# A down projection whose five weight pairs move on one at a time, with loads and epilogues placed by side

## The chip, the cores and the metric

The kernel runs on one core of one Trainium2 chip. The metric is device time in microseconds (us); lower is better. The engines are called PE (matrix multiply), DVE, ACT and POOL, and SP is the engine whose queue issues the transfers. Each engine has a queue of its own and works through it in order; engines wait for each other through semaphores.

## The reference

The program is one layer of a hybrid encoder in float32: a combined input projection, three mixers, an output projection with a norm, and a feed-forward. Only the feed-forward matters here:

```python
D_MODEL, SEQ, D_FF, N_META = 1024, 2048, 2816, 16
f = causal_dwconv(rms_norm(h, norm_ffn_pre[l]) @ ffn_up[l], ffn_conv[l])   # 3 taps
gate, val = jnp.split(f, 2, axis=-1)
f = (jax.nn.gelu(gate, approximate=True) * val) @ ffn_down[l]              # 2816 x 1024
h = h + rms_norm(f, norm_ffn_post[l])
return h[:, N_META:]
```

## The kernel before, in words

Float32 products are made of split operands. An operand is split into a rounded part and the remainder (`split`, L1593 to L1595: a copy on ACT, then a subtraction on DVE or, for some, on POOL), and a product is three matmuls of parts (`mm3`, L172 to L174).

**ffn_up** is the stage ahead. It works in three sweeps ("supers") over the tokens, each with 22 column blocks j. At the end of a block the convolution and the gelu (`conv`, L1723 to L1727, and `ending`, whose multiply is L1731) read the PSUM sums psu, and the result goes to the scratch tensor scr_ff (L1732). Between blocks the function `between` runs work for later; with j = `DOWN_FROM` in the last sweep it loads and splits the first operands of the next stage.

**The down projection** (class `Down` and the block `p4`) multiplies scr_ff by ffn_down. The tokens are cut into 8 pairs of 256. The 2816 rows of the weight are cut into 10 weight pairs of 256 rows (k = 0 to 9) and a rest of 256 rows. Each weight pair is multiplied in a scheme with 7 products in place of 8 (`DOWN_PRODUCTS`), for which both sides are summed in advance. So a weight pair has 7 operands of 128 x 512, each loaded (`down_operands`, L1814, tiles raw; four of the seven are sums that an earlier stage has written to scr_ds), split (on DVE, two of seven on POOL) and kept as a tile of two parts (dw, or qd for nine operands that lie in the memory of the norm's output).

The data side of one weight pair and one token pair is a *side* (`Down.side`): a load u (L1831), four POOL additions (L1838 to L1841), and a split into fo. Then come 21 matmuls, 7 products of 3. One token pair with five weight pairs is a *visit* (`Down.pair`). All 8 PSUM banks belong to this stage.

- First half: 8 visits with k = 0 to 4. All 35 operands stay resident. A visit ends with copies out of PSUM (L1870 to L1872), sums on DVE (L1873 to L1877, L1886) and the stores of the partial result to scr_part (L1894).
- Second half: 8 visits with k = 5 to 9, then the rest (tiles dwn, 24 matmuls). The 35 operands are replaced when the second half begins. The epilogue loads the partial sums (pt, L1881), adds them on POOL (L1883), adds the last PSUM banks (L1886), loads the residual (hx, L1902), applies the norm (`add_normed`, L1507 to L1523) and stores the result (L1904).

The order of instructions on each queue is set by a scheduler, which places each instruction as soon as its estimated inputs are ready; `issue_after` pins an instruction behind another. Pools of tiles are carved from one memory, and a new tile waits for the last readers of the memory that it takes. Raw operands have 8 buffers, u and fo two each, pt and hx together two.

Of the kernel before, what the change touches and what calls it, by code (L numbers as in the profile page):

```python
# [1526 lines left out]

HALO = 2
# [172 lines left out]
DOWN_SLOTS = 5, 13, 8  # L1701
DOWN_TURNS = (2, 3), (0, 5), (1, 13), (2, 5)
DOWN_FROM = 14
# [4 lines left out]
def ffn_up(core, raws, ring, pool, banks, w_up, cw, scr, between, tokens):  # L1708
# [11 lines left out]
    def conv(src, u, j, n):  # L1720
        y = pool.tile([P, FBLK], F32, tag="uy", name=core.n("uy"), bufs=UY)
        cc = u * NFF + j
        nc.scalar.activation(y[:, :n], src[:, 2 : n + 2], AF.Copy, scale=cw[:, 88 + cc : 89 + cc])  # L1723
        for i in (1, 0):
            stt(y[:, :n], src[:, i : n + i], cw[:, 44 * i + cc : 44 * i + cc + 1], y[:, :n], op0=ALU.mult, op1=ALU.add)  # L1725
        if u == 0:
            nc.scalar.activation(y[:, :n], y[:, :n], AF.Gelu_apprx_tanh)  # L1727
        return y
# [5 lines left out]
    for at, (sup, j) in enumerate(units):  # L1734
# [9 lines left out]
        for i, (name, (_, _, at_)) in enumerate(PRODUCTS.items()):  # L1744
# [20 lines left out]
            elif name == "p3":  # L1765
                tt(ps, ps, u2, op=ALU.add)
                gb = conv(ps, 0, j, n[1])
# [3 lines left out]
            elif name == "p2":  # L1771
                tt(ps, ps, ga, op=ALU.add)
                ga = conv(ps, 0, j, n[0])
                ending(gb, vb, j, b0[1], n[1])
            else:
                va = conv(ps, 1, j, n[0])
# [18 lines left out]


# [5 lines left out]
def down_operands(core, raw, slot, w_down, scr, k):  # L1802


    out = []
    for i, (_, s) in enumerate(DOWN_PRODUCTS.values()):
        t = raw()
# [13 lines left out]
class Down:  # L1821
    def __init__(self, core, spool, fpool, epool, psum, scr, gain, out):
        self.core, self.spool, self.fpool, self.epool, self.psum = core, spool, fpool, epool, psum
        self.scr, self.gain, self.out = scr, gain, out

    def side(self, k, pair):
# [4 lines left out]
        nc.sync.dma_start(u[:, 0:4].rearrange("p (j i) t -> p j (i t)", j=2), src.rearrange("(j p) t -> p j t", p=P))  # L1831
        if k == DOWN_PAIRS:
            fo = self.fpool.tile([P, 2, 4, P], F32R, tag="fo", name=core.n("fo"))
            split(core, fo[:, 0], fo[:, 1], u[:, 0:4])
            return {s: (fo[:, 0, i], fo[:, 1, i]) for i, s in enumerate(("b0", "a0", "b1", "a1"))}
        tt = nc.gpsimd.tensor_tensor
        b0, a0, b1, a1, s1, s2, s3, s4 = (u[:, i] for i in range(8))
        tt(s1, b0, b1, op=ALU.add)  # L1838
        tt(s2, s1, a0, op=ALU.subtract)
        tt(s3, a0, b0, op=ALU.subtract)  # L1840
        tt(s4, a1, s2, op=ALU.subtract)  # L1841
        fo = self.fpool.tile([P, 2, 7, P], F32R, tag="fo", name=core.n("fo"))
        split(core, fo[:, 0], fo[:, 1], u[:, 1:8])
        return {s: (fo[:, 0, i], fo[:, 1, i]) for i, s in enumerate(DOWN_SIDE)}
# [4 lines left out]
    def pair(self, pair, ks, weights, rest=None):  # L1849
# [3 lines left out]
        for k in ks:  # L1853
            side, w = self.side(k, pair), weights(k)
# [15 lines left out]
        nc.scalar.activation(la, ps["p1"][:], AF.Copy)  # L1870
# [7 lines left out]
        for i, row in enumerate(((lb, rb), (la, ra)) if rest else ()):  # L1878
            t0 = P * (2 * pair + i)
            pt = self.spool.tile([P, D], F32, tag="hx", name=core.n("pt"))  # L1880
            nc.sync.dma_start(pt[:], self.scr["part"][t0 : t0 + P, :])  # L1881
            for c, y in enumerate(row):
                nc.gpsimd.tensor_tensor(y, y, pt[:, 512 * c : 512 * c + 512], op=ALU.add)  # L1883
# [5 lines left out]
    def first(self, pair, ks, weights):  # L1889
        nc = self.core.nc  # L1890
        for i, halves in zip((1, 0), self.pair(pair, ks, weights)):
            t0 = P * (2 * pair + i)
            for c, y in enumerate(halves):
                nc.sync.dma_start(self.scr["part"][t0 : t0 + P, 512 * c : 512 * c + 512], y)  # L1894

    def second(self, pair, ks, weights, rest):
        core, nc = self.core, self.core.nc
        a, b, junk = self.pair(pair, ks, weights, rest)
        for i, halves in ((1, a), (0, b)):
            t0 = P * (2 * pair + i)  # L1900
            hx = self.spool.tile([P, D], F32, tag="hx", name=core.n("hx"))
# [312 lines left out]
```

## Time and profile before

| | |
|---|---|
| median of 3 runs | 3066.63 us |
| the runs | 3066.63, 3073.84, 3063.35 us |
| profiled execution: span | 3071.8 us (no separate time of it is given; the span is taken as its time) |
| mean granted clock of PE | 0.969 |
| PE busy | 95% of the span |
| matmuls of the down projection | 1872, from 2597.3 to 3060.6 us |

The profile is of one execution. Times within it are counted from the start of the span. The rows of the views follow where the prediction uses them. A row of a table by stretches has the length of the stretch, the busy time of each engine with the number of its instructions, the granted clock of PE (1.00 is full), the mean busy share of the DMA engines, and GB/s. A row of a table of waits has the engine and operation that waited, what it waited for, the total in us, how often, and the longest.

### The profile page before, as it was taken

To read this page: it belongs to the slowest core of one execution; us is meant where nothing else is said; L and a number is where in the kernel's file an instruction comes from. 1 tells how busy PE (TensorE), PEld (TensorE's weight loads), DVE (VectorE), ACT (ScalarE), POOL (GpSimd) and SP (SyncE) were. 2 spreads that over 40 slices of the span, in tenths; PEclk is the share of its full clock that TensorE was granted. 3 is DMA by queue.
4 is the path that set the end of the run, shared out by engine and by line. 5 is a ranking of instruction groups with operands and counts; after the bars stand their busy time and mean duration, and the time that the engine had idled before them with its cause. 6 is when DMAs were issued, how large, how long until landed. Compare 5 with 4: busy or idle time off the path is not lost. (4 is left out here: it accounts for less than half of the span.)

```text
span 3071.8 us, 52793 instructions
## 1 busy us (share of the span) xinstructions
PE 2921.6 (95%) x18694; PEld 2495.2 (81%) x18694; DVE 2054.8 (67%) x3934; ACT 1482.3 (48%) x2853; POOL 1358.8 (44%) x1589
## 2 busy tenths in 40 slices
PE   6999999999989999999989899999999999999998
PEld 6998898888876654665558899999999998787876
DVE  5268645656667785556635788888778786547766
ACT  4245332443336553555534656666566665324333
POOL 1001121122114555667842457445655444547765
PEclk9998999999988898999999999999999999999999
DMA  6776578466654346535245555566777765435444
GB/s 211 244 237 207 161 244 287 156 211 204 196 153 94 88 104 199 133 99 122 62 129 173 168 182 180 169 201 208 214 215 216 219 189 171 161 104 171 149 160 144
DMA packets 467818, 532.58 MB, mean 173 GB/s; under 512 B 85488, under 2 KB 355514, under 8 KB 466000
## 3 DMA queue, kind: packets, MB, share of 16 engines
q1 hardware_dynamic: 467168, 528.81, 56.5%
q8 instruction: 147, 2.41, 0.3%
q14 instruction: 119, 0.97, 0.1%
q0 software_dynamic: 384, 0.39, 0.0%
HBM read 369.11 MB, written 159.95 MB: 172 GB/s over the span
## 5 line engine op out<-in xcount | busy, mean ns | idle before, releaser
L172 PE MATMUL psu<-xo,uw 128*128 128x344 f32 x1848 | 589.9, 323 | 16.7 <-ACT xo L1594 6.9
L173 PE MATMUL psu<-xo,uw 128*128 128x344 f32 x1848 | 592.6, 321 | 0.0
L174 PE MATMUL psu<-xo,uw 128*128 128x344 f32 x1848 | 582.9, 320 | 0.0
L172 PE MATMUL psp<-xh,wh 128*128 128x384 f32 (+2 forms) x1152 | 383.6, 333 | 4.1 <-ACT wh L166 2.4
L174 PE MATMUL psp<-xh,wl 128*128 128x384 f32 (+2 forms) x1152 | 380.7, 331 | 3.5 <-DMA wl<-scr_wk 3.5
L173 PE MATMUL psp<-xl,wh 128*128 128x384 f32 (+2 forms) x1152 | 380.5, 330 | 0.0
L172 PEld LDWEIGHTS psu<-xo,uw 128*128 128x128 f32 x1848 | 346.9, 188 | 20.3 <-ACT xo L1594 7.1
L1595 DVE TENSOR_TENSOR uw<-uq,uw 128x512 fp32r<-128x512 f32 x341 | 316.2, 933 | 70.3 <-ACT uw L1594 63.7
L173 PEld LDWEIGHTS psu<-xo,uw 128*128 128x128 f32 x1848 | 347.9, 188 | 0.3 <-DVE xo L1595 0.3
L174 PEld LDWEIGHTS psu<-xo,uw 128*128 128x128 f32 x1848 | 346.5, 188 | 0.0
L1594 ACT ACTIVATE uw<-uq 128x512 fp32r<-128x512 f32 x462 | 287.9, 627 | 110.1 <-PE psu L174 48.7
L686 ACT ACTIVATE p<-sc,bias 128x512 f32<-128x512 f32 (+4 forms) x352 | 195.8, 590 | 178.5 <-PE sc L682 146.3
L1725 DVE SCALAR_TENSOR_TENSOR uy<-psu,ffn_cols,uy 128x342 f32<-128x342 f32 (+1 forms) x396 | 223.9, 567 | 60.7 <-ACT uy L1723 59.1
L559 DVE TENSOR_REDUCE mc<-mx 128x1 f32<-128x512 f32 (+6 forms) x352 | 190.3, 565 | 100.9 <-PE mx L554 75.8
L1731 POOL TENSOR_TENSOR uy<-uy,uy 128x342 f32<-128x342 f32 (+1 forms) x132 | 140.6, 1065 | 253.2 <-DVE uy L1725 77.4
L725 POOL TENSOR_TENSOR acc<-acc,p 128x512 f32<-128x512 f32 (+3 forms) x208 | 221.8, 1068 | 60.3 <-ACT p L686 23.9
L1595 POOL TENSOR_TENSOR uw<-uq,uw 128x512 fp32r<-128x512 f32 x121 | 177.9, 1470 | 125.0 <-ACT uw L1594 92.7
L174 PEld LDWEIGHTS psp<-xh,wl 128*128 128x128 f32 x1152 | 222.1, 193 | 13.0 <-issue 6.1
L172 PEld LDWEIGHTS psp<-xh,wh 128*128 128x128 f32 x1152 | 222.1, 193 | 10.7 <-issue 4.0
L173 PEld LDWEIGHTS psp<-xl,wh 128*128 128x128 f32 x1152 | 222.1, 193 | 7.6 <-issue 5.5
L1595 DVE TENSOR_TENSOR fo<-u,fo 128x896 fp32r<-128x896 f32 x88 | 112.6, 1279 | 121.3 <-ACT fo L1594 121.3
L1594 ACT ACTIVATE fo<-u 128x896 fp32r<-128x896 f32 x88 | 81.1, 922 | 206.3 <-POOL u L1841 106.8
(465 smaller groups left out, 6470.4 us busy)
## 6 DMA issues: line engine op xcount, KB each, us to landing
uq<-scr_us SPq DMA_DIRECT2D x220, 256.0 KB
uq<-in_ffn_up_dram SPq DMA_DIRECT2D x209, 256.0 KB
wl<-scr_wk SPq DMA_DIRECT2D x48, 512.0 KB
wh<-scr_wk SPq DMA_DIRECT2D x48, 512.0 KB
u<-scr_ff SPq DMA_DIRECT2D x88, 256.0 KB
scr_ff<-uy SPq DMA_DIRECT2D x110, 171.0 KB
raw<-in_w_in_dram SPq DMA_DIRECT2D x24, 512.0 KB
scr_wk<-wh SPq DMA_DIRECT2D x24, 512.0 KB
```

Source lines behind the costliest of these rows:

```text
L172: nc.tensor.matmul(out, ah, bh, start=first, stop=False, skip_group_check=more)
L173: nc.tensor.matmul(out, ah, bl, start=False, stop=False, skip_group_check=more)
L174: nc.tensor.matmul(out, al, bh, start=False, stop=last, skip_group_check=more)
L559: self.reduced = nc.vector.tensor_reduce(mc[:rows, i, ci : ci + 1], ps[:rows, : e - a], axis=AX.X, op=ALU.max)
L686: last = nc.scalar.activation(p[:rows, :w], ps[:rows, :w], AF.Exp, bias=bias[:rows, j : j + 1])
L725: eng.tensor_tensor(a, ps_[0][0][:rows, c0:n] if start and i == 1 else a, p[:rows, : n - c0], op=ALU.add)
L1594: core.nc.scalar.activation(hi, src, AF.Copy)
L1595: (eng or core.nc.vector).tensor_tensor(lo, src, hi, op=ALU.subtract)
L1725: stt(y[:, :n], src[:, i : n + i], cw[:, 44 * i + cc : 44 * i + cc + 1], y[:, :n], op0=ALU.mult, op1=ALU.add)
L1731: core.pooled = nc.gpsimd.tensor_tensor(v[:, :n], g[:, :n], v[:, :n], op=ALU.mult)
```

## The change

The five resident weight pairs become a window that slides. In the first half the windows of the eight visits begin at k = 0, 0, 1, 1, 2, 3, 3, 4, in the second at 5, 5, 6, 6, 7, 8, 8, 9, counted modulo 10; so a token pair p has the same window in both halves, shifted by five, and all ten pairs are used once. One weight pair is replaced at a time: 14 sets of seven operands are loaded and split, where it was 10. A set that the next visit needs is prepared from the third side of the visit before it (`ahead`, `DOWN_AHEAD`), in visits 1, 3, 4, 6, 7, 9, 11, 12 and 14 (of 0 to 15), and its loads are pinned behind the load u of that side.

Further parts:

- Ten operands (all of k = 0, three of k = 1) are prepared in ffn_up, at j = 13 and j = 17 of the last sweep, where it was seven; the tenth lies in the memory of ffn_up's norm gain. The loads of k = 2 and 3 are pinned behind the last convolution (`DOWN_HELD`).
- The convolutions of ffn_up's last block read copies in SBUF, not PSUM; this adds one copy on ACT.
- The weights of the rest are loaded in visit 6.
- Work behind a visit is put off, counted in sides, each piece pinned behind a side's u load: the stores of partial sums by 5, pt's loads and POOL's additions by 2, hx and the norm by 5, the store of the result by 7.
- In the second half the last PSUM banks are added before the stored partial sums instead of after them.
- The norm multiplies by the gain before the root is known, and adds the scaled row into hx in one operation (`add_scaled`).
- The pools of the stage are in another order, and their sizes are 5, 7, 1, 2 and 10 operands beside the nine and the tenth.

```diff
+def add_scaled(core, pool, halves, gain, x, junk):
+
+    nc = core.nc
+    v = pool.tile([P, 8], F32, tag="rs2", name=core.n("rs2"))
+    sums = v[:, 4:5], v[:, 5:6]
+    for y, acc in zip(halves, sums):
+        nc.scalar.activation(junk, y, AF.Square, accum_out=acc)
+    for c, y in enumerate(halves):
+        nc.vector.tensor_tensor(y, y, gain[:, 512 * c : 512 * c + 512], op=ALU.mult)
+    r1 = rstd_root(core, v, sums, D)
+    for c, y in enumerate(halves):
+        xc = x[:, 512 * c : 512 * c + 512]
+        nc.vector.scalar_tensor_tensor(xc, y, r1, xc, op0=ALU.mult, op1=ALU.add)
...
-DOWN_SLOTS = 5, 13, 8
-DOWN_TURNS = (2, 3), (0, 5), (1, 13), (2, 5)
-DOWN_FROM = 14
+DOWN_SLOTS = 5, 7, 1, 2, 10
+DOWN_TURNS = (3, 2), (4, 5), (0, 5), (4, 5), (1, 7), (2, 1)
+DOWN_FROM = 13, 17
+DOWN_HELD = 2, 4
+DOWN_REST = 6
+DOWN_AHEAD = 2
+DOWN_STORED = 5
+DOWN_PARTS, DOWN_NORMS, DOWN_OUT = 2, 5, 7
...
+                sum_ = ps if more else u2
+                tt(sum_, ps, u2, op=ALU.add)
+                gb = conv(sum_, 0, j, n[1])
             elif name == "p7":
                 tt(vb, ps, vb, op=ALU.add)
                 vb = conv(vb, 1, j, n[1])
             elif name == "p2":
-                tt(ps, ps, ga, op=ALU.add)
-                ga = conv(ps, 0, j, n[0])
+                sum_ = ps if more else ga
+                tt(sum_, ps, ga, op=ALU.add)
+                ga = conv(sum_, 0, j, n[0])
                 ending(gb, vb, j, b0[1], n[1])
             else:
-                va = conv(ps, 1, j, n[0])
+                src = ps
+                if not more:
+                    src = s("ga")
+                    nc.scalar.activation(src, ps, AF.Copy)
+                va = conv(src, 1, j, n[0])
...
+def down_visits(pairs):
+
+    for half in range(2):
+        for pair in range(pairs):
+            first = DOWN_CUT * pair // pairs + DOWN_CUT * half
+            yield half, pair, range(first, first + DOWN_CUT)
...
+    def after(self, sides, fn):
+        self.due.append((self.sides + sides, fn))
...
+        self.sides += 1
+        while self.due and self.due[0][0] <= self.sides:
+            with core.tc.issue_after(load.ins):
+                self.due.pop(0)[1]()
+        return side
+
+    def finish(self):
+        while self.due:
+            self.due.pop(0)[1]()
...
-        for k in ks:
-            side, w = self.side(k, pair), weights(k)
+        for i, k in enumerate(ks):
+            if i == DOWN_AHEAD:
+                self.due.insert(0, (self.sides + 1, ahead))
+            side, w = self.side(k % DOWN_PAIRS, pair), weights(k)
...
-        for i, row in enumerate(((lb, rb), (la, ra)) if rest else ()):
-            t0 = P * (2 * pair + i)
-            pt = self.spool.tile([P, D], F32, tag="hx", name=core.n("pt"))
-            nc.sync.dma_start(pt[:], self.scr["part"][t0 : t0 + P, :])
-            for c, y in enumerate(row):
-                nc.gpsimd.tensor_tensor(y, y, pt[:, 512 * c : 512 * c + 512], op=ALU.add)
...
+        self.after(DOWN_STORED, lambda: store(1, a))
+        self.after(DOWN_STORED, lambda: store(0, b))
...
+        def parts():
+            for t0, halves in rows:
+                pt = self.spool.tile([P, D], F32, tag="hx", name=core.n("pt"))
+                nc.sync.dma_start(pt[:], self.scr["part"][t0 : t0 + P, :])
+                for c, y in enumerate(halves):
+                    nc.gpsimd.tensor_tensor(y, y, pt[:, 512 * c : 512 * c + 512], op=ALU.add)
+
+        def norms():
+            for t0, halves in rows:
+                hx = self.spool.tile([P, D], F32, tag="hx", name=core.n("hx"))
+                nc.sync.dma_start(hx[:], self.scr["h"][META + t0 : META + t0 + P, :])
+                add_scaled(core, self.spool, halves, self.gain, hx, junk)
+                sums[t0] = hx
+
+        def stores():
+            for t0, hx in sums.items():
+                nc.sync.dma_start(self.out[t0 : t0 + P, :], hx[:])
+
+        self.after(DOWN_PARTS, parts)
+        self.after(DOWN_NORMS, norms)
+        self.after(DOWN_OUT, stores)
...
+        def slot():
+            down.append(down.pop(0))
+            home = down[-1]
+            return home.tile([P, 2, 512], F32R, tag="dw", name=core.n("dw")) if hasattr(home, "tile") else home
...
+                if j in DOWN_FROM:
                     raw = lambda: tmp.tile([P, 512], F32, tag="uq", name=core.n("raw"))[:]
-                    ws.append(down_operands(core, raw, lambda: down.pop(0), a["ffn_down"], scr, 0))
+                    k = DOWN_FROM.index(j)
+                    some = range(min(len(DOWN_PRODUCTS), len(down) - len(DOWN_PRODUCTS) * k))
+                    ws[k] = down_operands(core, raw, slot, a["ffn_down"], scr, k, some)
...
+        dws += [pool(p4, f"dw{i + 2}", n, **early) for i, n in enumerate(DOWN_SLOTS[2:])]
+        down[:0] = [dws[i] for i, n in DOWN_TURNS for _ in range(n)]
...
+        ended = core.taken.ins, core.conved.ins
+
+        def weights(c):
+            have = ws.setdefault(c, [])
+            if len(have) < len(DOWN_PRODUCTS):
+                raw = lambda: dwr.tile([P, 512], F32, tag="dq", name=core.n("raw"))[:]
+                with ExitStack() as behind:
+                    for ins in ended if c in range(*DOWN_HELD) else ():
+                        behind.enter_context(tc.issue_after(ins))
+                    some = range(len(have), len(DOWN_PRODUCTS))
+                    have += down_operands(core, raw, slot, a["ffn_down"], scr, c % DOWN_PAIRS, some)
+            return have
+
+        rest = []
 
         def last():
-            if not rest:
-                for i in range(2):
-                    rest.append(dwn.tile([P, 2, D], F32R, tag=f"r{i}", name=core.n("dwn")))
-                    at = P * (2 * DOWN_PAIRS + i)
-                    load_parts(core, (dpo, "hx", None), a["ffn_down"][at : at + P, :], rest[i][:, 0], rest[i][:, 1])
             return rest
 
-        rest = []
-        for pair in range(pairs):
-            steps.second(pair, ks[1], weights, last)
+        visits = list(down_visits(pairs))
+        for (half, pair, ks), following in zip(visits, visits[1:] + visits[-1:]):
+
+            def ahead(pair=pair, half=half, ks=ks, last=following[2][-1]):
+                if last not in ks:
+                    weights(last)
+                if half == 0 and pair == DOWN_REST:
+                    for i in range(2):
+                        rest.append(dwn.tile([P, 2, D], F32R, tag=f"r{i}", name=core.n("dwn")))
+                        at = P * (2 * DOWN_PAIRS + i)
+                        load_parts(core, (dpo, "hx", None), a["ffn_down"][at : at + P, :], rest[i][:, 0], rest[i][:, 1])
+
+            if half == 0:
+                steps.first(pair, ks, weights, ahead)
+                if pair == 1:
+                    gain = a["norm_ffn_post"].rearrange("(o n) -> o n", o=1).broadcast_to([P, D])
+                    nc.sync.dma_start(g_fpost[:], gain)
+            else:
+                steps.second(pair, ks, weights, ahead, last)
+        steps.finish()
```

100 lines of the change are left out of this document (41 added, 59 removed).

## The prediction

> **What bounds the kernel now.** I read the page first, then the groups of the accumulators psd (the matmuls of the down projection, L172 to L174), then a table of stretches with its borders at the visits, then PE's waits.
>
> ```profile
> span 3071.8 us, 52793 instructions
> PE 2921.6 (95%) x18694; PEld 2495.2 (81%) x18694; DVE 2054.8 (67%) x3934; ACT 1482.3 (48%) x2853; POOL 1358.8 (44%) x1589
> ```
>
> PE is busy for 95% of the span, and the change removes no matmul. So a gain can only come out of PE's idle or slow time, and the change touches only the last stage.
>
> ```profile
> L172 PE MATMUL psd<-dw,fo x416: 388/392/632, 2612.9 to 3054.4; 128*128 128x512 f32 x139
> L172 PE MATMUL psd<-qd,fo x144: 390/395/765, 2597.3 to 3035.4; 128*128 128x512 f32 x144
> ```
>
> (operation, count: duration in ns min/median/max, first and last start.) The stretches:
>
> ```profile
> 2597.30:2637.00 39.70, 31.24 (x107) 23.38 (x106) 26.14 (x30) 21.73 (x35) 21.80 (x26) 0.79 0.66 228
> 2637.00:2782.00 145.00, 145.00 (x631) 118.41 (x631) 68.85 (x81) 38.06 (x48) 75.06 (x121) 1.00 0.32 107
> 2782.00:2810.70 28.70, 24.86 (x107) 19.44 (x106) 24.90 (x25) 15.95 (x26) 23.38 (x22) 1.00 0.65 210
> 2810.70:2847.20 36.50, 33.56 (x130) 26.24 (x131) 29.68 (x31) 16.35 (x27) 26.61 (x31) 0.91 0.49 161
> 2847.20:2876.80 29.60, 29.60 (x130) 24.21 (x129) 22.07 (x29) 11.58 (x21) 19.43 (x24) 1.00 0.49 158
> 2876.80:3060.60 183.80, 181.29 (x775) 144.22 (x773) 127.20 (x163) 60.53 (x116) 122.14 (x140) 1.00 0.47 155
> 3060.60:3071.80 11.20, 0.12 (x1) 0.00 (x0) 6.76 (x14) 2.57 (x8) 0.94 (x1) 0.67 0.39 141
> ```
>
> Columns: stretch, length, then busy time and count of PE, PEld, DVE, ACT and POOL, the granted clock, DMA share and GB/s. A visit is 105 matmuls in the first half (7 products x 3 x 5 weight pairs) and 129 in the second (24 more for the rest). The second row holds six undisturbed visits: 145.0 us for 630 matmuls, 0.230 us each. By that pitch a visit should last 24.2 or 29.7 us, a side (one weight pair, 21 matmuls) 4.83 us. Lost against it: visit 0 39.7 - 24.2 = 15.5; visits 1 to 6 nothing; visit 7 28.7 - 24.2 = 4.5; visit 8 36.5 - 29.7 = 6.8; visit 9 nothing; visits 10 to 15 183.8 - 6 x 29.7 = 5.6. That is **32.4 us**, the ceiling of a gain; behind it is a tail of 11.2 us.
>
> ```profile
> PE psd L172 <- ACT fo L1594: 6.2, 7, 3.7
> PE psd L172 <- DVE uy L1725: 3.0, 1, 3.0
> PE psd L172 <- ACT uy L1727: 2.9, 1, 2.9
> PE psd L174 <- DVE fo L1595: 2.7, 2, 2.3
> PE psd L173 <- DVE dw L1595: 2.1, 1, 2.1
> PE psd L172 <- ACT dw L1594: 0.4, 1, 0.4
> ```
>
> These are PE's waits from 2597 to 3061 (total, times, longest). They sum to 17.3 us, about half of the 32.4. The rest is slow matmuls after a wait; columns: stretch, length, PE busy and count, clock, DMA:
>
> ```profile
> 2605.00:2610.00 5.00, 4.31 (x10) 0.50 0.94 336
> 2620.00:2625.00 5.00, 5.00 (x15) 0.58 0.84 285
> 2805.00:2810.00 5.00, 1.96 (x8) 1.00 0.85 272
> 2810.00:2815.00 5.00, 3.90 (x10) 0.69 0.97 328
> 2830.00:2835.00 5.00, 5.00 (x18) 0.76 0.31 100
> ```
>
> From 2605 to 2610, 10 matmuls filled 4.31 us where 2.3 would do: a wait of two to four us is followed by some 2 us lost to the clock. The waits of 0.6 us and less in visits 10 to 15 are not: that stretch has clock 1.00.
>
> **The change, part by part.**
>
> *The start (visits 0 and 1).* Now 35 operands have to be split within visit 0, of which 28 came late; the queue on SP (which issues all transfers in order) stood still meanwhile:
>
> ```profile
> 2592.54 0.32 SPq L1732 DMA_DIRECT2D scr_ff<-uy  x1
> 2596.60 0.32 SPq L1814 DMA_DIRECT2D raw<-scr_ds  x1
> 2601.25 0.81 SPq L1814 DMA_DIRECT2D raw<-in_ffn_down_dram  x2
> ```
>
> (SP's timeline: start, us.) The groups of operand splits in that stretch (busy, mean ns, idle before and what ended it):
>
> ```profile
> L1595 DVE TENSOR_TENSOR dw<-raw,dw 128x512 fp32r<-128x512 f32 x17 | 16.4, 990 | 4.8 <-ACT dw L1594 4.8
> L1594 ACT ACTIVATE dw<-raw 128x512 fp32r<-128x512 f32 x22 | 13.4, 626 | 8.6 <-DMA raw<-scr_ds 4.3 <-DMA raw<-in_ffn_down_dram 4.1
> L1595 POOL TENSOR_TENSOR dw<-raw,dw 128x512 fp32r<-128x512 f32 x8 | 11.2, 1394 | 12.9 <-ACT dw L1594 7.4 <-DMA scr_ff<-uy 5.5
> L167 DVE TENSOR_TENSOR dwn<-raw,dwn 128x1024 fp32r<-128x1024 f32 x2 | 2.5, 1227 | 1.6 <-ACT dwn L166 1.6
> L166 ACT ACTIVATE dwn<-raw 128x1024 fp32r<-128x1024 f32 x2 | 2.1, 1061 | 2.0 <-DMA raw<-in_ffn_down_dram 2.0
> ```
>
> After the change, visit 0 uses pairs 0 to 4 as before, but 10 operands instead of 7 are ready when it starts, visit 1 uses the same five, the splits stand in the order of their use on every queue, and the two loads, two ACT and two DVE splits of the rest (2.1 and 2.5 us) are gone to visit 6. What is left is 25 operands: ACT 25 x 0.626 = 15.7 us, DVE 17 or 18 x 0.99 = 17 to 18 beside 5 splits of u, POOL some 7 x 1.39 = 10. All fit into 24.2 us, but not early: the bytes are 25 x 256 KB = 6.6 MB, 20 us at the 336 GB/s of 2605 to 2610 and 29 us at the stretch's mean of 228. The two waits on uy (5.9 us, and 2 us each of slow clock behind them) are PSUM banks held by the last convolution. Its inputs are now copied to SBUF (one more ACT copy, near 0.6 us, and psu frees before the taps of L1725), so these go but for 0 to 1 us. The splits' own waits (2.5 us and 2 us of clock) shrink by the order, or come back where the DMA is late. I take 4 us lost in visits 0 and 1 together, between 2 (one PSUM wait and a late split) and 9 (the splits as late as today and one slow stretch).
>
> *The window.* Pairs are replaced one by one: 14 sets against 10 now, 28 more loads of 256 KB, 28 ACT splits (17.5 us in all), 20 DVE splits (19.8 us) and 8 POOL splits (11.2 us) by the rows above. They stand beside matmuls. In a first-half visit DVE, ACT and POOL now work 11.5, 6.3 and 12.5 of 24.2 us (a sixth of the second stretch); a set adds 5 x 0.99, 7 x 0.63 and 2 x 1.39. In the second half they work 21.2, 10.1 and 20.4 of 29.7 us, with a set 26.2, 14.5 and 23.2. No engine becomes the bound by its total; what remains is the order. A set's seven loads are pinned behind the third side's u (issued when the first side begins), and its 1.84 MB lands in 5.6 to 6.7 us by the 272 and 328 GB/s rows. ACT's queue has those seven copies ahead of the third side's fo, which is done another 0.6 + 0.9 + 1.3 us later: 8.4 to 9.5 us after the first side began, where the third begins at 9.7. So in the five weight visits of the first half (1, 3, 4, 6, 7) nothing is lost in the middle case: 1 us in all, 0 to 6.
>
> Visit 6 takes the rest's loads and splits too (2.1 us of ACT, 2.5 of DVE); with 24.2 us and those totals it still fits, and is the likeliest of the five to lose something. The partial sums' stores, put off by five sides, leave SP free for the loads and hold la to ra longer, by about one visit of 24.2 us, in which nothing else writes them before its end.
>
> *The switch (visits 7 and 8).* No 35 operands change hands: 11.3 us lost now, 0.5 after (0 to 3).
>
> *The second half.* Here the third side waits already:
>
> ```profile
> L1594 ACT ACTIVATE fo<-u 128x896 fp32r<-128x896 f32 (+1 forms) x35 | 31.3, 895 | 67.7 <-POOL u L1841 57.6 <-PE psd L174 10.1
> L1840 POOL TENSOR_TENSOR u<-u 128x128 f32<-128x128 f32 x28 | 30.9, 1102 | 0.0
> L1883 POOL TENSOR_TENSOR la<-la,pt 128x512 f32<-128x512 f32 x6 | 10.0, 1669 | 6.3 <-DVE u L1873 6.3
> L1595 DVE TENSOR_TENSOR fo<-u,fo 128x896 fp32r<-128x896 f32 (+1 forms) x35 | 45.0, 1284 | 29.2 <-ACT fo L1594 29.2
> ```
>
> (groups of 2876.8 to 3060.6), and SP's own waits from 2847 on (total, times, longest):
>
> ```profile
> SPq L1902 <- POOL ra L1883: 62.5, 8, 9.5
> SPq L1831 <- DVE fo L1595: 48.3, 26, 2.4
> ```
>
> POOL's four adds of the stored part (up to 1.67 us each) stand ahead of a side's four u operations, and SP waits up to 9.5 us to issue hx (L1902), with the u loads of L1831 behind it. The change puts both behind later u loads, so visits without a set (8, 10, 13, 15) lose 0.3 instead of 0.9 each. In the four with a set (9, 11, 12, 14) ACT's queue has, beside the seven copies, four squares (128x512 too, so some 0.63 us each by the split's row) that wait for POOL's adds; they make the third side 0 to 2.4 us late. I take 1.3 us, nearer the middle: 4 x 1.3 + 4 x 0.3 = 6.4 us, between 2 and 14 (each set's visit at 3.2).
>
> *The tail.*
>
> ```profile
> 3058.61 1.69 POOL lb L1883
> 3060.30 1.25 POOLq L2210
> 3061.57 0.69 DVE rb L1886
> ...
> 3066.62 0.60 DVE hx L1523
> ```
>
> (Chain: start, us, what.) The PSUM adds now come before POOL's, which saves DVE 0.69 us behind the last POOL add; the gain is multiplied in while the sum of squares is taken, and hx is loaded after POOL's adds instead of before. I take -0.4 us, between -1.5 and +1.
>
> *Elsewhere.* Up to the last ffn_up third every queue holds the same instructions in the same order: 0. The wider pool on the feed-forward's left moves no transfer past another there.
>
> Sum of what is lost after: 4 + 1 + 0.5 + 6.4 = 11.9 us against 32.4, so 20.5 gained, and 0.4 in the tail: **21 us**. On the profiled 3071.8 that is 3051. This execution is 5.2 us above the median of the three runs (3066.6), inside their 3063 to 3074, so against the median I say **3046 us**.
>
> **A rule weighed.** The rows price a stall at its wait plus some 2 us where it is 2.1 us or longer (the 2.1 us on dw is followed by clock 0.58 in 2620 to 2625). The Trainium skill, page "TensorE: Matmul & The Clock Gate", section "What's actually happening", says that the clock halves only after an idle window of about 3.4 us. This trace disagrees: waits of 2.1 to 3.0 us led to half speed here. By the page a stalled weight visit would cost its wait alone and the second rival below would give 3056 instead of 3064.
>
> **The rivals.**
> 1. *The start is bound by the transfers.* For it: 0.94 of DMA at 2605 to 2610, and 6.6 MB needing 20 to 29 us. Against it: SP stood still from 2592.9 to 2601.2. Visits 0 and 1 then lose 12 instead of 4: gain 13, **3054 us**.
> 2. *The sets stall the second half.* For it: ACT's fo waits 57.6 us on POOL there already, and POOL's add took 1.67. Each of the four visits loses 4 + 2 (wait and clock): 24 + 1.2 + 4 + 1.5 = 30.7 lost, gain 2, **3064 us**: no change.
> 3. *Slower: a u load behind seven pinned loads.* SP has one order. If the seven wait for a raw buffer or a slot whose pair PE still reads, the next side's u waits with them, in all nine weight visits. With 4 + 1.2 + 0.5 lost elsewhere, the change stops paying from 27.1 / 9 = 3.0 us per weight visit (3066.6), and is slower by over 0.3% from 4.0. A 3 us wait with its 2 us of clock is 5.0: 45 + 5.7 = 50.7 lost, **3085 us**. For it: L1831 waits 48.3 us in the second half now. Against it: a set is due a visit later, eight raw buffers hold seven loads, and a side's u is loaded two sides ahead.
>
> **The numbers.** Forecast 0.60, rival 1 0.12, rival 2 0.14, rival 3 0.14. What a measurement can tell is 0.3%, 9 us: faster is below 3057. Faster: 0.60 and most of rival 1, 0.70; within: rival 2 and the rest of 1, 0.16; slower: 0.14. The forecast's own range: lost 2 + 0 + 0 + 2 = 4 gives 3038, lost 9 + 3 + 1 + 10 = 23 gives 3057. The stated range leaves rival 3 out: 3036 (tail 1.5 better) to 3070 (rival 2 and the spread of runs).
>
> **What would show it.** Right: psd's first visit near 27 us with no wait on uy; visits 7 and 8 at 24.2 and 29.7 us; the third sides of 9, 11, 12 and 14 with waits on fo of 1 to 2 us, clock 1.00. Wrong: clock under 0.9 in the weight visits (rivals 2, 3), SP's u loads waiting on raw or dw (3), ACT's splits waiting on raw transfers up to 2625 (1).

## The result, and the profile after

The changed kernel takes 3073.37 us in the median of 22 runs (3068.27 to 3083.34), the kernel before 3069.71 us in 22 runs beside it (3063.35 to 3077.75). The ratio is 1.0018, with a 95% interval of 1.001 to 1.0026: **0.2% slower**, where 0.7% faster was forecast.

The profiled executions seem to say otherwise: the span after is 3070.1 us, 1.7 us shorter. But the down projection's first matmul comes at 2590.2 us instead of 2597.3, behind stages of which the change touches only the end of ffn_up. In the fourteen profiles of this study that start lies between 2588.2 and 2606.1 us, with no relation to what was changed behind it. So the stage is compared by its own length, from its first matmul to the end of the span: 474.5 us before, 479.9 after, 5.4 us more, which fits the ratio (0.18% of 3069.71 is 5.5 us) and leaves nothing clear for the stages ahead.

The stage after, cut at the visits 0 and 1, 2 to 6, 7 and 8, 9 to 15, and the tail (columns as in the prediction):

```profile
2590.20:2648.10 57.90, 52.61 (x213) 38.30 (x212) 40.48 (x44) 30.68 (x50) 37.36 (x43) 1.00 0.64 211
2648.10:2770.10 122.00, 121.32 (x527) 98.50 (x526) 74.97 (x86) 46.81 (x65) 73.97 (x106) 1.00 0.45 152
2770.10:2823.90 53.80, 53.80 (x235) 44.01 (x234) 33.53 (x38) 17.40 (x24) 31.49 (x45) 1.00 0.44 149
2823.90:3057.40 233.50, 216.57 (x904) 173.32 (x902) 169.06 (x210) 87.78 (x163) 148.84 (x171) 0.97 0.50 171
3057.40:3070.10 12.70, 0.08 (x1) 0.00 (x0) 7.44 (x13) 2.65 (x8) 3.34 (x3) 0.61 0.44 165
```

At 0.230 us a matmul these stretches should last 48.3, 120.8, 53.8 and 207.7 us. "Lost" is what a stretch lasts beyond that, here and in all that follows:

| lost, us | before | forecast | after |
|---|---|---|---|
| visits 0 and 1 | 15.5 | 4 | 9.6 |
| visits 2 to 6 | 0 | 1 (with 1 and 7) | 1.2 |
| visits 7 and 8 | 11.3 | 0.5 | 0 |
| visits 9 to 15 | 5.6 | 6.4 (with 8) | 25.8 |
| tail, its length | 11.2 | 10.8 | 12.7 |

The switch is gone, as forecast. The start gained half of what was forecast. The second half lost 20 us more, and that ate both.

How far one profile can be trusted shows where a stretch is the same in several kernels. Visits 9 to 15 lose 25.8 us here and 26.0 in an experiment that changes only the first half. Visits 0 and 1 lose 9.0 to 11.1 us in this kernel and in the six experiments that change only the second half. So a difference of two us between two profiles says little.

By visits (9 to 15, PE alone; columns: length, PE busy and count, clock, DMA):

```profile
2823.90:2855.90 32.00, 30.39 (x131) 1.00 0.51 175
2855.90:2890.80 34.90, 31.40 (x131) 0.95 0.50 166
2890.80:2922.60 31.80, 30.39 (x131) 1.00 0.52 184
2922.60:2958.90 36.30, 31.52 (x131) 0.95 0.62 202
2958.90:2988.70 29.80, 29.80 (x130) 1.00 0.45 150
2988.70:3023.50 34.80, 31.46 (x130) 0.95 0.54 185
3023.50:3057.40 33.90, 31.61 (x130) 0.95 0.36 129
```

A visit should take 29.7 us. Visits 10 and 15 take 34.9 and 33.9, and no weight set is prepared in them; visit 13, also without one, takes 29.8. All of PE's waits in this stretch, and the three largest groups of the start (2590 to 2649):

```profile
PE psd L172 <- ACT fo L1611: 16.9, 6, 4.8
```

```profile
PE psd L173 <- DVE dw L1612: 1.6, 4, 0.7
PE psd L172 <- ACT fo L1611: 1.5, 2, 0.9
PE psd L172 <- DVE la L1936: 0.9, 1, 0.9
```

The first row is six waits, one in each visit but 13, all at the third side. The other 8.9 of the 25.8 us are slower matmuls behind them (the four longest waits are in the visits with clock 0.95). What stands ahead of that side's fo is on POOL's queue: in all six, ACT begins fo within 0.1 us of the end of its u operations. Visit 12 begins at 2922.6, its third side is due at 2932.2 (POOL's timeline: start, us):

```profile
2924.12 1.31 POOL L1962 TENSOR_TENSOR la<-la,pt 128x512 f32<-128x512 f32 x1
2925.39 2.14 POOL L1962 TENSOR_TENSOR ra<-ra,pt 128x512 f32<-128x512 f32 x1
2927.49 1.75 POOL L1962 TENSOR_TENSOR lb<-lb,pt 128x512 f32<-128x512 f32 x1
2929.20 0.91 POOL L1883 TENSOR_TENSOR u<-u 128x128 f32<-128x128 f32 x1
2930.07 0.91 POOL L1885 TENSOR_TENSOR u<-u 128x128 f32<-128x128 f32 x1
2930.95 1.74 POOL L1962 TENSOR_TENSOR rb<-rb,pt 128x512 f32<-128x512 f32 x1
2932.64 0.92 POOL L1884 TENSOR_TENSOR u<-u 128x128 f32<-128x128 f32 x1
2933.51 1.71 POOL L1612 TENSOR_TENSOR dw<-raw,dw 128x512 fp32r<-128x512 f32 x1
2935.18 0.90 POOL L1886 TENSOR_TENSOR u<-u 128x128 f32<-128x128 f32 x1
```

L1883 to L1886 (from 2929.20 on) are the third side's four u operations, L1962 the additions of the stored partial sums, L1612 a split of the new set. The u operations take 3.6 us, and 8.7 us of other work is put ahead of and between them. In the kernel before these additions stood ahead of the last PSUM additions and began while PE still did the rest's matmuls. Of the visit that ends at 2907.5 us this is the second one:

```profile
2906.67 1.30 POOL L1883 TENSOR_TENSOR ra<-ra,pt 128x512 f32<-128x512 f32 x1
```

It began 0.8 us before the next visit. After the change the second addition comes behind the PSUM additions, at 2925.39, 2.8 us into the visit: 3.6 us later.

Visit 13 shows that the additions are not all of it. It has the same four, 7.0 us in all, and loses 0.1. Its third side's u was loaded early, so that two of its u operations came in ahead of the second addition (SP's and POOL's timelines; the visit begins at 2958.9):

```profile
2955.79 6.02 SPq L1873 DMA_DIRECT2D u<-scr_ff  x2
2959.58 0.46 POOL L1883 TENSOR_TENSOR u<-u 128x128 f32<-128x128 f32 x1
```

This load waits for its buffer, until DVE has split the first side's fo. Counted from each visit's first matmul it is issued:

| visit | 9 | 10 | 11 | 12 | 13 | 14 | 15 |
|---|---|---|---|---|---|---|---|
| third side's u load, us | -1.7 | +0.4 | -2.1 | +0.3 | -3.1 | -0.6 | -0.8 |
| lost, us | 2.3 | 5.2 | 2.1 | 6.6 | 0.1 | 5.1 | 4.2 |

By and large, the later the load, the more is lost. A late load alone costs little: with the additions on DVE (below), it is issued 0.8 us into visit 15, which loses 0.3. The load's time was not varied alone.

### The profile page after: what moved, and what is told of

It is laid out like the page before. It is cut to its first block, busy times and chain, and to the rows that moved or that the text cites. A ratio compares the mean times of both kernels' runs of the same rounds, so it can differ in the third digit from the quotient of the medians.

```text
span 3070.1 us, 52890 instructions
## 1 busy us (share of the span) xinstructions
PE 2909.4 (95%) x18694; PEld 2485.8 (81%) x18694; DVE 2075.9 (68%) x3954; ACT 1498.2 (49%) x2882; POOL 1370.7 (45%) x1597
## 4 chain that ended last, share of the span: by engine, by line
PE 36%; DMA 5%; POOL 3%; DVE 3%; issue 2%; ACT 1%; SPq 0%; POOLq 0%; DVEq 0%; ACTq 0%
PE psu L172 8%; PE psu L173 8%; PE psu L174 8%; PE psd L172 3%; PE psd L173 2%; PE psd L174 2%; DMA u<-scr_ff 2%; DMA xt<-scr_h 1%; PE pswo L174 1%; PE pswo L172 1%; PE pswo L173 1%; DVE uw L1612 1%; POOL u L1883 0%; DVE uy L1747 0%; POOL u L1885 0%
## 5 line engine op out<-in xcount | busy, mean ns | idle before, releaser
L1612 DVE TENSOR_TENSOR uw<-uq,uw 128x512 fp32r<-128x512 f32 x341 | 313.7, 926 | 68.2 <-ACT uw L1611 65.7
L1612 POOL TENSOR_TENSOR uw<-uq,uw 128x512 fp32r<-128x512 f32 x121 | 180.3, 1490 | 122.7 <-ACT uw L1611 93.4
L172 PEld LDWEIGHTS psp<-xh,wh 128*128 128x128 f32 x1152 | 221.1, 192 | 10.9 <-issue 4.0
L1611 ACT ACTIVATE fo<-u 128x896 fp32r<-128x896 f32 x88 | 81.1, 922 | 202.2 <-POOL u L1886 120.8
L1612 DVE TENSOR_TENSOR fo<-u,fo 128x896 fp32r<-128x896 f32 x88 | 103.8, 1184 | 100.9 <-ACT fo L1611 100.7
```

The costliest lines, as they stand in the source:

```text
L172: nc.tensor.matmul(out, ah, bh, start=first, stop=False, skip_group_check=more)
L1611: core.nc.scalar.activation(hi, src, AF.Copy)
L1612: (eng or core.nc.vector).tensor_tensor(lo, src, hi, op=ALU.subtract)
```

## The experiments

Four explanations were set against each other: **A**, POOL's additions stand ahead of a side that is needed; **B**, the new weight sets cost it (the forecast's second and third rivals); **D**, the gain multiplications, moved beside the additions, make them slow; **E**, the start is bound by the operands' transfers. C and A' are named in the expectations that use them. Line numbers are those of each kernel; "lost" as above. Where no ratio is given, there is one execution, the profiled one.

**The additions one side later** (one constant).

```diff
-DOWN_PARTS, DOWN_NORMS, DOWN_OUT = 2, 5, 7
+DOWN_PARTS, DOWN_NORMS, DOWN_OUT = 3, 5, 7
```

> One constant of the changed kernel: the loads of the stored partial sums and POOL's four additions are put off by three sides instead of two, so that on POOL's queue the third side's u operations stand ahead of the additions. Theory A (the additions, 5.2 to 7 us of POOL that can begin only behind the last PSUM additions, stand ahead of the third side's u operations): the waits of PE at the third sides of visits 9 to 15, 16.9 us in the changed kernel, fall under 4 us, matmul time lost in visits 9 to 15 falls from 26 to under 8 us, and the time by about 18 us. Theory B (the new weight sets of the second half cost it: splits on ACT and POOL, seven loads on SP): the waits at the third sides of visits 9, 11, 12 and 14 stay (over 10 us), the time moves by under 8 us. Theory C (the additions only move the same collision to the fourth side): the waits stay above 12 us in sum, at fourth sides.

It became slower: ratio 1.0084 (1.006 to 1.0108), 44.2 us lost in visits 9 to 15. Visits 10 and 11 of this kernel, and PE's waits in 9 to 15:

```profile
2868.50:2898.60 30.10, 30.10 (x131) 1.00 0.46 155
2898.60:2939.50 40.90, 32.13 (x130) 0.87 0.50 164
```

```profile
PE psd L172 <- ACT fo L1611: 33.6, 4, 8.8
```

Visits without a set lose 0.4 to 0.6 us now, as A says; the four with a set lose 8.9 to 11.5 each, at the fourth side, as C says. There the additions wait in POOL's queue behind two splits of the set, which wait for ACT's copies and their loads, and the fourth side's u operations wait behind all six. In visit 11 that side's u also lands late, 12.1 us into the visit, since its load is issued behind the set's and pt's loads (the third rival's picture); POOL then holds it for another 5.3 us. Neither the additions nor the sets are harmless where both share a queue with u.

**The additions left out.**

```diff
-                for c, y in enumerate(halves):
-                    nc.gpsimd.tensor_tensor(y, y, pt[:, 512 * c : 512 * c + 512], op=ALU.add)
```

> POOL's additions of the stored partial sums are left out of the changed kernel (so the second half's results lack the first half); their loads stay. Theory A: the matmul time lost in visits 9 to 15 falls from 26 to under 6 us. Theory B: the four visits with a weight set (9, 11, 12, 14) still lose 2 us or more each, over 10 us together.

```profile
2832.90:3040.50 207.60, 207.60 (x904) 1.00 0.58 197
```

Visits 9 to 15 lose nothing, and the execution took 3051.68 us (3073.58 for the kernel before beside it). The sets alone, with all loads and all splits, cost the second half nothing: B by itself falls.

**The window held still**, the rest as changed.

```diff
-            first = DOWN_CUT * pair // pairs + DOWN_CUT * half
+            first = DOWN_CUT * half
```

> The changed kernel with the window held still: pairs 0 to 4 in every visit of the first half, 5 to 9 in the second, so 10 sets instead of 14 and all 35 operands change at visit 8; all else as changed. Theory A: visits 9 to 15 lose as much as in the changed kernel, at least 18 of 26 us, since the additions stand where they stood; visits 7 and 8 lose some 8 to 12 us again; visits 0 and 1 lose 12 to 16 us (all 28 operands in visit 0). Theory B: visits 9 to 15 lose under 10 us.

Visits 7 and 8, and 9 to 15:

```profile
2771.90:2836.60 64.70, 58.12 (x235) 0.95 0.69 234
2836.60:3057.00 220.40, 211.22 (x904) 0.99 0.44 147
```

Visits 7 and 8 lose 10.9 us again, so the window does save the switch. Visits 9 to 15 lose 12.7 us, between the two expectations: with no set in them the late additions cost half of what they cost beside the sets. Visits 0 and 1 lose 6.8 us, where 12 to 16 were expected: a miss.

**The additions where they were**, ahead of the last PSUM additions, the rest as changed.

```diff
+        for i, row in enumerate(((lb, rb), (la, ra)) if rest else ()):
+            t0 = P * (2 * pair + i)
+            pt = self.spool.tile([P, D], F32, tag="hx", name=core.n("pt"))
+            nc.sync.dma_start(pt[:], self.scr["part"][t0 : t0 + P, :])
+            for c, y in enumerate(row):
+                nc.gpsimd.tensor_tensor(y, y, pt[:, 512 * c : 512 * c + 512], op=ALU.add)
         for y, name in ((la, "p2"), (ra, "p3"), (lb, "p4"), (rb, "rb")):
...
-DOWN_PARTS, DOWN_NORMS, DOWN_OUT = 2, 5, 7
+DOWN_PARTS, DOWN_NORMS, DOWN_OUT = 2, 5, 6
...
-        self.after(DOWN_PARTS, parts)
```

> The changed kernel with the stored partial sums loaded and added on POOL where the kernel before does it: inside the visit, ahead of the last PSUM additions (the result's store is put off by 6 sides instead of 7, so that its buffer is free). The norms stay put off. Theory A: the additions begin during the rest's matmuls again, so visits 9 to 15 lose near what they lost before, 5 to 10 us instead of 26; the time falls by 15 to 20 us. Theory B: visits 9 to 15 lose over 16 us.

Ratio 1.0037 (1.002 to 1.0054); visits 9 to 15 lost 29.7 us. PE's two largest groups of waits there:

```profile
PE psd L172 <- ACT fo L1611: 11.7, 15, 0.9
PE psd L172 <- DVE ra L1942: 4.1, 6, 0.8
```

A miss for A. B's bound (over 16) is met, but B by itself has fallen above. The long waits became many short ones: PSUM banks are held again until POOL has added (the second row), and in one visit's chain the gain multiplications stand on DVE between those additions and a split of fo. At the second sides ACT begins fo 1.0 us after its u is ready, at the third sides of the weight visits 3.3 us after: it is still busy with the norm. So undoing this one step does not bring the old times back, and no run isolates the additions' place from the steps that moved around it.

**The additions spread**, one behind the u operations of each of four sides (`parts` only loads pt now; `summed` is a side's last u operation).

```diff
-        self.after(DOWN_PARTS, parts)
+        def add():
+            y, part = adds.pop(0)
+            with core.tc.issue_after(self.summed.ins):
+                nc.gpsimd.tensor_tensor(y, y, part, op=ALU.add)
...
+        self.after(2, parts)
+        for sides in (2, 3, 4, 5):
+            self.after(sides, add)
```

> The changed kernel with POOL's four additions of the stored partial sums spread: one behind the u operations of each of the second to fifth sides that follow (each pinned behind that side's last u operation), where all four stood behind the second side's u load; all else as changed. Theory A (four additions in a row ahead of a side's u operations cost the second half its 26 us; leaving them out took the loss to 0.3): one addition of 1.3 to 2.1 us fits into the slack of a side of 4.83 us beside u operations of 2 to 3.6 us, visits 9 to 15 lose under 6 us, and the time is 12 to 22 us below the kernel before. Theory A' (the split operations of the sets on POOL need the remaining slack): the weight visits 9, 11, 12 and 14 still lose 2 us or more each, the others under 0.5; the time is 5 to 12 us below the kernel before.

```profile
2829.10:3061.20 232.10, 217.10 (x904) 0.98 0.52 172
```

Another miss: ratio 1.0031 (1.0018 to 1.0044), 24.4 us lost, in visits with and without a set (4.5 us in visit 15, 0.2 in visit 10). But POOL's u operations are no longer what comes last. In nine of the ten waits on fo, ACT begins fo 1.9 to 3.9 us after its u is ready: one of the norm's squares stands ahead of it on ACT's queue and waits for an addition. The fifth side of visit 9 (POOL's last u operation, then ACT's square and fo):

```profile
2846.91 0.79 POOL L1886 TENSOR_TENSOR u<-u 128x128 f32<-128x128 f32 x1
2848.99 0.63 ACT L1534 ACTIVATE u<-rb 128x512 f32<-128x512 f32 x1 [4.41 <-POOL rb L1968]
2849.62 0.93 ACT L1611 ACTIVATE fo<-u 128x896 fp32r<-128x896 f32 x1
```

So this is what the prediction feared of the squares, and it came when the additions were moved out of u's way. At the third sides of visits 11, 12 and 14 a set's copies stand behind the square as well. Which part of the 24.4 us is whose was not tried.

**The additions on DVE.**

```diff
-                    nc.gpsimd.tensor_tensor(y, y, pt[:, 512 * c : 512 * c + 512], op=ALU.add)
+                    nc.vector.tensor_tensor(y, y, pt[:, 512 * c : 512 * c + 512], op=ALU.add)
```

> The changed kernel with the four additions of the stored partial sums on DVE instead of POOL. Theory A: POOL then never stands between a side's u and PE for longer than a split, and four DVE additions of 0.7 us (0.95 beside POOL) bring DVE to some 29 of 29.7 us in a weight visit; visits 10, 13 and 15 lose under 1 us each, the four weight visits 1 to 4 us each as DVE becomes late with fo; the time is 8 to 18 us below the kernel before. If DVE's load is the true limit of the second half, visits 9 to 15 lose over 20 us.

Visits 9 to 15:

```profile
2828.10:3038.80 210.70, 208.77 (x904) 169.01 (x902) 171.39 (x239) 87.65 (x163) 110.81 (x140) 1.00 0.56 189
```

3054.59 us against 3066.06 beside it: ratio **0.9959** (0.9943 to 0.9975), **faster than both kernels**. Visits 9 to 15 lose 3.0 us. POOL falls from 148.8 to 110.8 us there, and DVE rises by only 2.3 us (169.1 to 171.4) for 28 more additions. What it does beside a less busy POOL takes less time: the medians of the gain multiplications, by operand, are 0.68 to 0.94 us, 0.95 to 1.59 in the changed kernel. A holds; the weight visits lose 0 to 1.6 us each, less than the 1 to 4 expected.

**The norm as before**, gain multiplied after the root; still put off.

```diff
-                add_scaled(core, self.spool, halves, self.gain, hx, junk)
+                add_normed(core, self.spool, halves, P, self.gain, hx, [junk] * 2)
```

> The changed kernel with the norm as before: the gain is multiplied in after the root, in two operations per half, instead of while the squares are taken; still put off by five sides. Theory D (the gain multiplications on DVE, which now run beside POOL's additions, stretch them from 1.3 to 1.7 and 2.1 us and so make the loss): POOL's additions fall to a mean near 1.35 us and visits 9 to 15 lose under 16 us instead of 26. If only their place counts, visits 9 to 15 lose over 20 us.

Visits 9 to 15 of this kernel, then the second addition on POOL (ns min/median/max) in the changed kernel and in this one:

```profile
2832.30:3056.40 224.10, 213.19 (x904) 0.98 0.53 178
```

```profile
L1962 POOL TENSOR_TENSOR ra<-ra,pt x8: 1301/1724/2155, 2824.1 to 3056.1; 128x512 f32<-128x512 f32 x8
```

```profile
L1962 POOL TENSOR_TENSOR ra<-ra,pt x8: 1293/1301/2182, 2832.2 to 3055.1; 128x512 f32<-128x512 f32 x8
```

16.4 us lost instead of 25.8, just beyond the bound that D had set. So the rewritten norm, which leaves DVE two operations a row behind the root instead of four, costs 9 us here. D's reason for it is not shown. The median of this one addition falls from 1.72 to 1.30 us, but the mean of all 28 additions only from 1.61 to 1.55, where 1.35 was expected: 1.7 us less in sum. What else the norm's order moves was not separated.

**One set for the first half.** Weight pair 0's operands stand in for pairs 1 to 4.

```diff
         def weights(c):
+            c = 0 if c < DOWN_CUT else c
```

> The changed kernel with the operands of weight pair 0 used in the place of pairs 1 to 4 too, so that no operand is loaded or split in visit 0 beyond the seven that were ready (the first half's sums are then of the wrong weights). Theory E (the start is now bound by the loads of 25 operands, 6.6 MB, at 0.88 to 1.05 of the DMA engines): visits 0 and 1 lose under 2 us instead of 9.7. If PSUM banks held by the last convolution or the first u loads cost it, they lose 4 us or more.

```profile
2602.50:2651.30 48.80, 48.80 (x212) 1.00 0.39 125
```

Visits 0 and 1 lose 0.5 us: without the 25 operands, loaded and split, the start costs nothing. The PSUM banks of the last convolution and the u loads by themselves cost nothing any more. Part of the 9.6 us needs the next set as well, which is prepared in visit 1: that visit loses 2.5 to 5.1 us in the seven kernels with this first half, and 1.0 in the two with the window held still.

**No splits on POOL.**

```diff
-DOWN_POOLED = (2, 5)
+DOWN_POOLED = ()
```

> The changed kernel with all operand splits on DVE (two of seven were on POOL); the additions of the stored partial sums stay on POOL. Theory A (the additions alone are too late for the third side): visits 10 and 15, which have no set, lose what they lost (5.3 and 4.2 us), the weight visits lose 1 to 2 us less each: 18 to 24 us in visits 9 to 15. Theory A' (the splits between the u operations make up much of it): visits 9, 11, 12 and 14 fall from 16.4 to under 6 us together.

```profile
2838.70:3075.40 236.70, 216.58 (x904) 0.96 0.50 168
```

29.0 us lost, more than the 25.8 with them, and more than the 18 to 24 that A expected. The four weight visits lose 13.8 together, not under 6: A' falls as the main cause. The additions remain ahead of u, and DVE has more to do (PE waits 2.4 us for its part of fo, in two waits).

**The gain's load out of the start**, on top of the additions on DVE: the transfer of 512 KB is issued in visit 2 instead of visit 0.

```diff
                 if last not in ks:
                     weights(last)
+                if half == 0 and pair == 2:
+                    gain = a["norm_ffn_post"].rearrange("(o n) -> o n", o=1).broadcast_to([P, D])
+                    nc.sync.dma_start(g_fpost[:], gain)
...
-                if pair == 1:
-                    gain = a["norm_ffn_post"].rearrange("(o n) -> o n", o=1).broadcast_to([P, D])
-                    nc.sync.dma_start(g_fpost[:], gain)
```

> The version with the additions on DVE (15 to 16 us of matmul time lost in the whole stage, 11 of them in visits 0 and 1), and the load of the norm's gain (512 KB, issued in visit 0 so far) put into visit 2, behind the third side's u. If the start is bound by transfers (25 operands of 256 KB, the gain, u): 0.5 MB less in visit 0 is some 1.5 us at 340 GB/s, visits 0 and 1 lose 9 to 10.5 instead of 11.2 us, and the time is 0.4 to 0.6% below the kernel before. If the splits themselves bound it, they lose 11 us as before.

```profile
2599.40:2659.60 60.20, 53.87 (x212) 0.94 0.61 199
```

Visits 0 and 1 lose 11.9 us instead of 11.1; ratio 0.9964 (0.9946 to 0.9982), as without it. No gain is seen, but the 0.7 to 2.2 us that were expected are no more than the spread of the start (9.0 to 11.1 us), so this does not rule the transfers out. Whether loads or splits order the start stays open.

**The window held still, additions on DVE.**

```diff
-            first = DOWN_CUT * pair // pairs + DOWN_CUT * half
+            first = DOWN_CUT * half
...
-                    nc.gpsimd.tensor_tensor(y, y, pt[:, 512 * c : 512 * c + 512], op=ALU.add)
+                    nc.vector.tensor_tensor(y, y, pt[:, 512 * c : 512 * c + 512], op=ALU.add)
```

> The version with the additions on DVE, and the window held still (10 sets, all 35 operands change at visit 8). The window itself: visits 7 and 8 lose 8 to 12 us instead of 0.1, the weight visits' 3.4 us go (visits 11 and 12 lose under 0.5 us), visits 0 and 1 lose 7 instead of 11 us; in sum 4 to 6 us more lost than with the window. If the window is worth nothing, the sums are equal within 2 us.

Visits 7 and 8, then 9 to 15:

```profile
2778.00:2843.60 65.60, 57.72 (x235) 0.95 0.70 233
2843.60:3051.30 207.70, 207.70 (x904) 1.00 0.47 156
```

11.8 us lost at the switch, nothing after it, 7.0 in visits 0 and 1: 18.8 in the stage, against 15.2 with the window. By these two profiles the window itself is worth 3.6 us: it saves 11.8 at the switch, and gives back 3.0 in the second half, 4.1 in visits 0 and 1 and 1.1 in 2 to 6. With the spread of the start it may be 2 us more.

**The kernel before, with its additions on DVE.**

```diff
-                nc.gpsimd.tensor_tensor(y, y, pt[:, 512 * c : 512 * c + 512], op=ALU.add)
+                nc.vector.tensor_tensor(y, y, pt[:, 512 * c : 512 * c + 512], op=ALU.add)
```

> The kernel before with its four additions of the stored partial sums on DVE instead of POOL, nothing else. Its visits 10 to 15 lost 5.6 us to fo waiting on POOL's u operations behind these additions: they fall to under 2 us if theory A holds there too, and the time falls by 3 to 6 us (0.1 to 0.2%). If DVE is then late with fo, they lose more than 6 us.

Its visits 9 to 15:

```profile
2840.10:3058.90 218.80, 211.65 (x904) 1.00 0.46 151
```

11.1 us lost instead of 5.6; ratio 1.0012 (0.9998 to 1.0026): no gain. In that kernel the additions stand ahead of the PSUM additions and, on DVE's queue, of the next side's fo. Moving them to DVE paid in the changed kernel, which puts them off, and not here.

## Why the prediction was wrong

- **The switch** (0.5 forecast): right, 0. Held still, it costs 10.9 to 11.8 us.
- **The window's first half** (1 forecast): right for visits 2 to 7, which lost 1.2, all of it in visit 6, the likeliest by the prediction. Visit 1 is counted with the start; its set costs time there. In visits 3, 4 and 7 an ACT queue with seven copies ahead of fo was as harmless as worked out.
- **The start** (4, between 2 and 9): mis-sized, 9.6. The PSUM waits went as forecast, the clock stayed at 1.00 in this execution, and one set used five times shows that without the operands nothing is lost. The first rival (12 lost) said that their transfers bind the start; whether it is the transfers or the splits is not shown. That visit 1, with a set of its own, would still be paying for them was not in the sum.
- **The second half** (6.4, between 2 and 14): the step that failed, 25.8. The sentence "The change puts both behind later u loads, so visits without a set (8, 10, 13, 15) lose 0.3 instead of 0.9 each" was wrong. A pin behind a u *load* on SP orders the loads; it does not put POOL's additions behind the u *operations*. The change also made the additions wait for the last PSUM additions, which in visit 12 run from 0.2 to 2.7 us into the visit. That wait was named nowhere: the working counts the new order only as a saving in the tail. Visits 10 and 15 lost 5.2 and 4.2 us instead of 0.3; visit 13 lost 0.1, its u having been loaded early.
- In the weight visits, ACT's four squares were named as what makes fo late. In the changed kernel POOL's u came last: in visits 11, 12 and 14 ACT had done its squares and copies and stood idle for 1.25, 1.46 and 2.02 us before fo. (Leaving the additions out took the loss to 0, but it also ends the squares' waits, so it does not tell the two apart.) The squares would have been next: in the version with the additions spread they are what holds fo. The price used, 1.67 us an addition, was near the truth (1.28 to 2.15); their place was not.
- **The rewritten norm** was costed at its saving in the tail only. It costs 9 us in the second half, for a reason that is not shown.
- **The tail** (-0.4): +1.5. Its additions end later for the same reason, 3.3 us behind the last matmul instead of 0.9, and hx is loaded into pt's buffers, so it lands after them (the first row covers POOL's last addition, the second is hx's load):

```profile
3059.07 1.68 POOLq L2293
3060.77 3.67 DMA hx<-scr_h
```

- **The rivals.** The second, no change with the sets stalling the second half, came out nearest (3064 forecast), and for a different reason: sets alone stall nothing, though beside them the additions cost twice as much. The third, SP's u loads behind seven pinned loads, did not happen by itself: with the additions left out, all seven loads and all u loads are in place and nothing is lost.

## What to carry to other kernels

Work that is put off must be placed on the queue of the engine that does it: a pin on the transfer that feeds it says nothing of what it will stand ahead of. The same holds for what reads its result: a square that waits for an addition holds up all that stands behind it on ACT. When an epilogue's order is turned round, list for each of its operations the last thing that it now waits for, and which operation of the next step stands behind it on the same engine. Where a helper engine feeds the critical one, filler on that engine needs slack within each step, not in the total: POOL was 64% busy in visits 9 to 15.

## What the runs showed of the hardware

**What slows a POOL addition.** In visit 12 the first addition (128 x 512, from 2924.12) takes 1.31 us and the second (from 2925.39) 2.14. DVE's work beside them:

```profile
2924.60 0.67 DVE L1936 TENSOR_TENSOR rb<-rb,psd 128x512 f32<-128x512 f32 x1
2925.20 1.18 DVE L1612 TENSOR_TENSOR fo<-u,fo 128x896 fp32r<-128x896 f32 x1
2926.30 1.78 DVE L1536 TENSOR_TENSOR la<-la,g_fpost 128x512 f32<-128x512 f32 x1
```

Beside DVE operations with one operand in PSUM (L1936) POOL keeps its time; beside those with two operands in SBUF (L1612, L1536) both are slowed, DVE's gain multiplication to 1.78 us (the same operation's minimum in this kernel is 0.69). The Trainium skill, page "GPSIMD Engine Reference", section "1. Specifications", says that GpSimd shares its SBUF interfaces with VectorE and contends with instructions that have two SBUF inputs; the trace agrees, and gives the price. All 32 additions of the changed kernel fit: the 14 with at most 0.5 us of such DVE work beside them took 1.28 to 1.31 us, the other 18 took 1.70 to 2.15.

**How long a wait halves the clock.** Two waits of the version with the additions spread, and the 5 us behind each (clock in the third column from the right):

```profile
2916.22 0.51 PE L172 MATMUL psd<-qd,fo 128*128 128x512 f32 x1 [1.86 <-ACT fo L1611]
3003.87 0.51 PE L172 MATMUL psd<-qd,fo 128*128 128x512 f32 x1 [1.85 <-ACT fo L1611]
```

```profile
2916.20:2921.20 5.00, 4.98 (x21) 1.00 0.78 283
3003.80:3008.80 5.00, 4.93 (x15) 0.66 0.20 56
```

Waits of the same length, and only one is followed by slow matmuls: 15 fill 4.93 us, where 21 would fit, 1.5 us more than the wait. So the prediction's bound of 2.1 us is no sharp one. In the fourteen profiles no wait of the down projection up to 1.78 us, with no other near it, lowered the clock. From 1.85 to 2.64 us some did and some did not (2.64 us in the kernel with the norm as before left it at 1.00), and all from 2.84 us on did. Two shorter waits close together can do it as well: 0.91 and 1.38 us within 2.4 us, in visit 1 of the same version, were followed by 0.66.
